# A decoder layer's output projection as seven products of halved matrices, with the summed and split weights made in the first SwiGLU's second phase

## The chip, the cores and the metric

The kernel runs on one core of one Trainium2 chip. The engines are TensorE (PE, matrix products), VectorE (DVE), ScalarE (ACT), GpSimd (POOL) and SyncE (SP, which here only issues transfers). The metric is the device time of one execution in microseconds. The kernel before takes 2163.99 us (median of 3 runs, 2163.88 to 2165.24).

## The reference, cut to what matters

```python
for l in range(DEPTH):                                  # DEPTH 1; x is 1 x 1024 x 1024, f32
    x = x + 0.5 * swiglu(rmsnorm(x, ffn1_norm[l]), ffn1_w_gu[l], ffn1_w_down[l])
    h = rmsnorm(x, mix_norm[l])
    z = h @ w_in[l]
    ...                                                 # y_a, y_b, y_c: three branches
    gates = jax.nn.sigmoid(z[..., COL_GATE:] + b_gate[l]).reshape(B, S, N_BRANCH, D_MODEL)
    merged = (gates[:, :, 0] * (y_a @ w_branch_a[l])
              + gates[:, :, 1] * (y_b @ w_branch_b[l])
              + gates[:, :, 2] * (y_c @ w_branch_c[l]))
    x = x + merged @ w_out[l]                           # the output projection, 1024 x 1024
    x = x + 0.5 * swiglu(rmsnorm(x, ffn2_norm[l]), ffn2_w_gu[l], ffn2_w_down[l])
```

## The kernel before

All activations are kept transposed: features on the 128 partitions, the 1024 tokens along the free dimension, in two halves of 512. A product of f32 matrices is three matmuls (`mm3`, L154): both operands are split into a rounded part (`whi`, a cast on ACT) and the rest (`wlo`, a subtraction on DVE), and the products hi by hi, hi by lo and lo by hi are summed in PSUM. `split` (L138) records such a cast and subtraction. A result of 128 x 512 fills one PSUM bank; there are four `bank` and four `one` (L127, taken by `single`).

The layer runs in stages: the first SwiGLU (`up` and `units`, then `down`), the gates' and latents' projections (`gates`), the three branches (`mixer`), the output projection (`project`), the second SwiGLU.

`down` (L2071) is the second phase of a SwiGLU. It computes a product of quartered matrices as seven loops (`loops`: b11, t3, t1, t2, b22, b21, t4), each of six steps `(n, s)`; five steps have two k tiles (24 matmuls of 512 columns) and one has one. Each step fetches the tiles of a later step (`fetch`: SP loads, `w_down` at L2109 and the other operand from `tdt` or `tdb` at L2111), splits the next step's operands (`prepare`, lines L139 and L142 in `split`), and runs what `acts` and `post` hang on it. `pre` and `post` carry the norm that follows and the start of the gates: `gates.first` (a load) and `gates.sums` (four additions on DVE). In this phase PE, SP, DVE and ACT run in the order of the code.

`mixer` (L1060) ends with sixteen products of the last branch, which fill `merged`, split into two parts as they come. `project` then makes sixteen outputs (2 halves x 8 blocks of 128 features), each a sum over 8 k tiles: 24 matmuls. For each it loads one 512 KB block of `w_out`, splits it, adds the bank to the residual (L1138) and feeds the norm: `norm.feed` squares on ACT and adds up on DVE (L1290). When half 0 is done, its norm is spread over the next outputs as `tasks`: `turned_sums` (four transposes on PE, L410, and a sum on DVE, L413), the steps of an inverse square root on DVE (L169 to L192, tiles `rms_v` and `rs_`), `norm_scale` (four transposes on PE, L425), and the product with the gains (L1327). Half 1's sums go by PE alone (L394). The order there is set by a scheduler for all engines.

## Time and profile before

| | |
|---|---|
| median of 3 runs | 2163.99 us (2163.88 to 2165.24) |
| profiled execution | 2163.42 us, span 2161.7 us |
| PE busy | 2152.9 us, 100% of the span |
| DVE, ACT, POOL busy | 1571.5, 911.7, 259.1 us |
| granted clock | 1.00 |
| data moved | 340.96 MB, 158 GB/s over the span |

Times in the trace are from the start of the span. The second phase of the first SwiGLU has its loop 2 from 499.5 us on and its loop 3 from 529.4. The last branch's sixteen products start at 1395.6, and the projection ends with the L425 transposes of half 1's norm at 1532.2. The page of the profile gives busy time, share and instructions for each engine, a map of 40 slices, the chain of work that ended last, and the costliest groups of instructions; a timeline row gives start, duration, engine, line, operation, output and inputs, and in square brackets the idle time before it and what ended it.

### The profile page before, as it was taken

The page shows a single profiled execution, that of the slowest core. Times are in us where ns is not written, and L with a number is a line of the kernel's source. Part 1 is how long each engine was busy: PE and PEld are TensorE (multiplying, and loading weights), DVE is VectorE, ACT ScalarE, POOL GpSimd, SP SyncE. Part 2 cuts the span into 40 slices and gives each one's busy share as a digit, 9 for nine tenths or more (in the row PEclk, how much of TensorE's full clock was granted, in tenths as well). Part 3 has the DMA queues.
Part 4 walks back from the last instruction along what each step waited for, and adds up shares of the span by engine and source line. Part 5 has one row for each costly group of instructions (what it writes and reads, how often), then busy time and mean ns, then how long its engine had stood idle before and what let it go on. Part 6 is the DMA issues. An engine that isn't in the chain of part 4 may idle for free.

```text
span 2161.7 us, 27485 instructions
## 1 busy us (share of the span) xinstructions
PE 2152.9 (100%) x10136; PEld 1798.9 (83%) x10136; DVE 1571.5 (73%) x2371; ACT 911.7 (42%) x1492; POOL 259.1 (12%) x268
## 2 busy tenths in 40 slices
PE   9999999999999999999999999999999999999999
PEld 6888888888887888888988899988888888888887
DVE  8966666679889657655886588876876666657884
ACT  6433333333455434443555378833433223224332
POOL 0011111100000000000123312240011212110000
PEclk9999999999999999999999999999999999999999
DMA  4264555385332444641687821192133332348543
GB/s 148 93 222 168 182 176 175 130 317 186 124 116 103 145 166 174 222 149 61 222 286 251 320 84 59 67 345 106 40 127 103 112 96 97 105 145 286 169 130 103
DMA packets 129975, 340.96 MB, mean 158 GB/s; under 512 B 15281, under 2 KB 23601, under 8 KB 129841
## 3 DMA queue, kind: packets, MB, share of 16 engines
q1 hardware_dynamic: 129696, 339.21, 45.5%
q8 instruction: 79, 1.29, 0.2%
q14 instruction: 56, 0.45, 0.1%
q10 hardware_dynamic: 144, 0.00, 0.0%
HBM read 229.33 MB, written 109.84 MB: 157 GB/s over the span
## 4 chain that ended last, share of the span: by engine, by line
PE 94%; DVE 4%; ACT 1%; issue 1%; DMA 0%; POOL 0%; ACTq 0%; POOLq 0%; DVEq 0%
PE one L158 15%; PE one L159 15%; PE one L160 15%; PE bank L158 13%; PE bank L159 13%; PE bank L160 13%; PE mm L158 2%; PE mm L159 2%; PE mm L160 2%; PE bank L1018 1%; PE bank L1033 1%; PE bank L1034 1%; PE bank L450 1%; DVE wlo L147 1%; PE bank L1950 1%; PE one L1950 1%
## 5 line engine op out<-in xcount | busy, mean ns | idle before, releaser
L146 ACT CAST whi<-x 128x1024 fp32r<-128x1024 f32 x202 | 192.2, 954 | 414.2 <-DVE x L1426 170.5
L147 DVE TENSOR_TENSOR wlo<-x,whi 128x1024 fp32r<-128x1024 f32 x202 | 241.3, 1196 | 59.2 <-ACT whi L146 19.4
L1454 DVE TENSOR_TENSOR t<-t,one 128x512 f32<-128x512 f32 x188 | 128.8, 685 | 192.3 <-PE one L160 192.2
L158 PE MATMUL bank<-h,whi 128*128 128x512 f32 x636 | 247.9, 390 | 0.0
L160 PE MATMUL bank<-h,wlo 128*128 128x512 f32 x636 | 247.5, 389 | 0.0
L159 PE MATMUL bank<-h,whi 128*128 128x512 f32 x636 | 247.5, 389 | 0.0
L158 PE MATMUL one<-h,whi 128*128 128x512 f32 x508 | 198.4, 391 | 0.0
L160 PE MATMUL one<-h,wlo 128*128 128x512 f32 x508 | 197.7, 389 | 0.0
L159 PE MATMUL one<-h,whi 128*128 128x512 f32 x508 | 197.7, 389 | 0.0
L158 PE MATMUL one<-w,whi 128*128 128x512 f32 x432 | 168.7, 390 | 0.1
L159 PE MATMUL one<-w,whi 128*128 128x512 f32 x432 | 168.1, 389 | 0.0
L160 PE MATMUL one<-w,wlo 128*128 128x512 f32 x432 | 168.1, 389 | 0.0
L142 DVE TENSOR_TENSOR wlo<-w,whi 128x1024 fp32r<-128x1024 f32 (+2 forms) x112 | 114.3, 1036 | 65.4 <-ACT whi L139 65.1
L139 ACT CAST whi<-w 128x1024 fp32r<-128x1024 f32 (+2 forms) x112 | 98.8, 902 | 148.5 <-PE one L159 63.9
L2050 POOL TENSOR_TENSOR raw<-raw 128x512 f32<-128x512 f32 x38 | 56.9, 1498 | 793.5 <-DVE raw L1891 685.0
L160 PEld LDWEIGHTS bank<-h,wlo 128*128 128x128 f32 x636 | 119.4, 188 | 25.0
L158 PEld LDWEIGHTS bank<-h,whi 128*128 128x128 f32 x636 | 119.4, 188 | 24.6
L159 PEld LDWEIGHTS bank<-h,whi 128*128 128x128 f32 x636 | 119.4, 188 | 24.4
L160 PE MATMUL bank<-whi,wlo 128*128 128x512 f32 x352 | 136.9, 389 | 0.0
L158 PE MATMUL bank<-whi 128*128 128x512 f32 x352 | 136.9, 389 | 0.0
L159 PE MATMUL bank<-wlo,whi 128*128 128x512 f32 x352 | 136.9, 389 | 0.0
L160 PEld LDWEIGHTS one<-h,wlo 128*128 128x128 f32 x508 | 95.3, 188 | 19.9
(406 smaller groups left out, 4902.7 us busy)
## 6 DMA issues: line engine op xcount, KB each, us to landing
x<-in_ffn_w_gu_dram SPq DMA_DIRECT2D x78, 512.0 KB, 5.1
w<-tdt SPq DMA_DIRECT2D x40, 512.0 KB, 4.6
gate<-raw SPq DMA_DIRECT2D x33, 512.0 KB, 3.0
tdb<-raw SPq DMA_DIRECT2D x64, 256.0 KB, 2.1
h<-in_ffn_w_down_dram SPq DMA_DIRECT2D x64, 256.0 KB, 6.0
w<-tdb SPq DMA_DIRECT2D x30, 512.0 KB, 4.5
tdt<-w SPq DMA_DIRECT2D x48, 256.0 KB, 2.3
x<-in_w_gate_dram SPq DMA_DIRECT2D x22, 512.0 KB, 7.0
```

What stands on the lines that cost most here:

```text
L139: i = self.nc.scalar.copy(hi, src)
L142: return (eng or self.nc.vector).tensor_tensor(lo, src, hi.bitcast(F32), op=ALU.subtract)
L146: self.nc.scalar.copy(hi, src)
L147: return lambda: self.nc.vector.tensor_tensor(lo, src, hi.bitcast(F32), op=ALU.subtract)
L158: i = mmul(out, s[0], m[0], start=first, stop=False, **kw)
L159: mmul(out, s[0], m[1], start=False, stop=False, **kw)
L160: self.last = mmul(out, s[1], m[0], start=False, stop=last, **kw)
L450: nc.tensor.transpose(b[:m, k * P:(k + 1) * P], s, self.ident)
L1018: nc.tensor.transpose(b[:, at:at + P], prs[t][:, kk * P:(kk + 1) * P], self.ident)
L1454: return self.nc.vector.tensor_tensor(out, x, y, op=ALU.add)
L1950: k.last = nc.tensor.matmul(b, w, norm.x(half, c), start=c == 0, stop=c == DT - 1)
L2050: sub = lambda d, x, y: (eng or nc.gpsimd).tensor_tensor(d, x, y, op=ALU.subtract)
```

## The change

Three things change. First, `merge` takes the place of `project`. It cuts `merged` (b11, b12, b21, b22) and `w_out` into quarters and makes seven products of four blocks with four k tiles each, 48 matmuls a product. Sums of quarters (t1 to t4) are made on DVE; product 1 (`p1`) is copied out of PSUM by ACT and added to the residual by POOL where it is needed; the others are added by DVE straight from PSUM (L1210), two of them after accumulating a second product in the same banks. PE's order in it is the code's; the other engines are ordered by the scheduler. The halves of the residual are stored and loaded the other way round.

Second, the seven weight matrices are made earlier. `out_jobs` makes fourteen jobs, two for each product. A job loads one quarter's half (512 KB), adds up to three further quarters with accumulating transfers issued by POOL, and four steps later splits the tile and stores both parts to `wo` in HBM. Job i starts at step 4 + i * 5 // 3 of the first SwiGLU's `down`, counted six to a loop. `merge` loads the parts back, 28 loads of 512 KB. Third, `gates.first(0)` and `gates.sums(0)` go from loop 1 to loop 5, and half 0's norm takes `one` banks for its transposes.

```diff
...
-        merged = [self.hrows() for _ in range(2)]
-        for _ in self.branch_pairs(
-                1, yb, mc, None, each, lambda d, f, x: self.split(*merged[f][d], x)):
-            pass
-        return merged
-
-    def project(self, merged, norm, sink):
-
...
+        return yb, mc
+    def out_jobs(self):
+        self.wo = self.dram.tile([7, 2, 2, P, D], F32, name="wo")
+        A11, A12, A22, A21 = range(4)
+        parts = ((A11,), (A11, A21, A22), (A21, A22), (A11, A21, A22, A12), (A11, A21), (A12,), (A22,))
+        def job(n, g):
+            x = self.raw()
+            src = self.a["w_out"][g]
+            self.nc.sync.dma_start(x, src[parts[n][0]])
+            for i in parts[n][1:]:
+                self.nc.gpsimd.dma_start(x, src[i], accum_op=ALU.add)
+            yield
+            hi = self.wide("whi")
+            lo = x.bitcast(F32R)
+            self.split(hi, lo, x)
+            for d, t in zip(self.wo[n, g], (hi, lo)):
+                self.nc.sync.dma_start(d, t.bitcast(F32))
+            yield
+        jobs = [job(n, g) for n in range(7) for g in range(2)]
+        when = {}
+        for i, j in enumerate(jobs):
+            q = 4 + i * 5 // 3
+            for at, k in ((q, 1), (q + 4, 0)):
+                at = when.setdefault((at // 6, at % 6), [])
+                at.insert(0 if k == 0 else len(at), lambda j=j: next(j))
+        return when
+    def merge(self, yb, mc, room, norm, load, sink):
+        nc, tt, h4 = self.nc, self.nc.vector.tensor_tensor, self.h4
+        names = ("b11", "b12", "b22", "b21")
+        raw = {n: [room() for _ in range(2)] for n in names}
+        w, op, x, banks = {}, {}, norm.x, {}
+        def put(name, p, src):
+            hi, lo = h4(F32R), h4(F32R)
+            op.setdefault(name, {})[p] = (hi, lo)
+            self.split(hi, lo, src)
+        def branch(name, k):
+            top, col = name[1] == "2", name[2] == "2"
+            dt, hf = 4 * top + k, int(col)
+            if dt not in w:
+                y = self.load(self.a["w_branch"][1, dt // 2])
+                w[dt], w[dt + 1] = y[:4], y[4:]
+            if k % 2 == 0:
+                branch.sig = self.x4()
+                for i in range(2):
+                    nc.sync.dma_start(branch.sig[:, i], self.sig[DT + dt + i][:, hf])
+            sig, m = branch.sig[:, k % 2], self.row()
+            nc.sync.dma_start(m, mc[dt][:, hf])
+            b = self.bank()
+            self.branch(b, w[dt], yb, hf)
+            tt(sig, sig, b, op=ALU.mult)
+            nc.gpsimd.tensor_tensor(raw[name][k // 2][:, k % 2], sig, m, op=ALU.add)
+        def weights(n):
+            out = []
+            for g in range(2):
+                ts = self.wide("whi"), self.wide("wlo")
+                for t, src in zip(ts, self.wo[n, g]):
+                    nc.sync.dma_start(t.bitcast(F32), src)
+                out += [tuple(t[:, u * 512:u * 512 + 512] for t in ts) for u in range(2)]
+            return out
+        def product(key, take, ws, name, first, last=True):
+            if first:
+                banks[key] = [None] * 4
+            for u in range(4):
+                if first:
+                    banks[key][u] = take()
+                for k in range(4):
+                    m = tuple(t[:, k % 2] for t in op[name][k // 2])
+                    s = tuple(t[:, k * P:(k + 1) * P] for t in ws[u])
+                    self.mm3(banks[key][u], s, m, first and k == 0, k == 3, skip_group_check=True)
+                yield u, banks[key][u]
+        def add(half, c, b, sign=ALU.add, parts=1):
+            y = x(half, c)
+            for n in self.parts(parts):
+                tt(y[:, n], y[:, n], b[:, n], op=sign)
+        for k in range(4):
+            branch("b11", k)
+            if k % 2:
+                put("b11", k // 2, raw["b11"][k // 2])
+        for k in range(4):
+            branch("b12", k)
+        ws = weights(0)
+        for k in range(4):
+            branch("b22", k)
+            if k % 2:
+                p = k // 2
+                b11, b12, b22 = (raw[n][p] for n in ("b11", "b12", "b22"))
+                tt(b12, b12, b22, op=ALU.subtract)
+                tt(b11, b12, b11, op=ALU.subtract)
+                put("t2", p, b11)
+        for k in range(4):
+            branch("b21", k)
+        load()
+        p1 = []
+        w2 = weights(1)
+        for u, b in product("a", self.single, ws, "b11", True):
+            p1.append(self.row())
+            nc.scalar.copy(p1[u], b)
+        for p in range(2):
+            b11, b22 = raw["b11"][p], raw["b22"][p]
+            put("b22", p, b22)
+            nc.vector.scalar_tensor_tensor(b22, in0=b22, scalar=-1.0, in1=b11, op0=ALU.mult, op1=ALU.subtract)
+        for p in range(2):
+            put("t1", p, raw["b22"][p])
+        ws = weights(2)
+        for u, b in product("x", self.bank, w2, "t2", True):
+            add(1, 2 * u + 1, b, ALU.subtract)
+        for u in range(4):
+            nc.gpsimd.tensor_tensor(x(0, 2 * u), x(0, 2 * u), p1[u], op=ALU.add)
+        for p in range(2):
+            put("t3", p, raw["b12"][p])
+        w2 = weights(3)
+        for u, b in product("x", None, ws, "t1", False):
+            add(0, 2 * u + 1, b, ALU.subtract)
+        for u in range(4):
+            nc.gpsimd.tensor_tensor(x(0, 2 * u + 1), x(0, 2 * u + 1), p1[u], op=ALU.subtract)
+        for p in range(2):
+            put("b21", p, raw["b21"][p])
+            tt(raw["b21"][p], raw["b21"][p], raw["b11"][p], op=ALU.add)
+        ws = weights(4)
+        for u, b in product("x", None, w2, "b22", False):
+            add(0, 2 * u, b)
+            norm.feed(0, 2 * u)
+        for u in range(4):
+            nc.gpsimd.tensor_tensor(x(1, 2 * u + 1), x(1, 2 * u + 1), p1[u], op=ALU.subtract)
+        for p in range(2):
+            put("t4", p, raw["b21"][p])
+        w2 = weights(5)
+        for u, b in product("y", self.bank, ws, "t3", True):
+            add(0, 2 * u + 1, b)
+            norm.feed(0, 2 * u + 1)
+            sink(0, 2 * u + 1)
+        ws = weights(6)
+        tasks, norm.take = [None, *norm.first()], self.single
+        for u, b in product("a", None, w2, "b21", False):
+            add(1, 2 * u, b)
+            norm.feed(1, 2 * u)
+            if u:
+                tasks[u]()
+        for u, b in product("y", None, ws, "t4", False):
+            parts = 2 if u == 3 else 1
+            if u == 0:
+                tasks[4]()
+                norm.take = None
+            add(1, 2 * u + 1, b, parts=parts)
+            norm.feed(1, 2 * u + 1, parts)
+            sink(1, 2 * u + 1)
...
-                    {(1, 0): [do(gates.first, 0)], (1, 4): [do(gates.sums, 0)],
+                    {(5, 0): [do(gates.first, 0)], (5, 2): [do(gates.sums, 0)],
                      (5, 3): [do(norm.high, 0), do(norm.low, 0)], (5, 4): [do(norm.apart, 0), do(gates.first, 1)],
...
-                    late)
+                    late, self.out_jobs())
...
-            merged = self.mixer(latents)
+            yb, mc = self.mixer(latents)
...
-            for half in range(2):
-                for p in range(DT // 2):
-                    nc.sync.dma_start(rows.take(half, p), x1d[half, p])
             norm = OpNorm(self, rows, lambda: self.g_ffn2)
             ffn = SwiGLU(self, a["ffn2_w_gu"], a["ffn2_w_down"], fp, norm, 2)
-            for f in range(2):
-                ffn.fetch(f, [ffn.w4] * 4)
-            self.project(merged, norm, lambda half, c: keep(x2d, norm.t, half, c))
+            def load():
+                for half, p in ((1, 0), (1, 1), (1, 2), (1, 3), (0, 0), (0, 1), (0, 2), (0, 3)):
+                    nc.sync.dma_start(rows.take(half, p), x1d[1 - half, p])
+            def sink(half, c):
+                if (half, c) == (0, 1):
+                    ffn.fetch(0, [ffn.w4] * 4)
+                elif (half, c) == (0, 3):
+                    ffn.fetch(1, [ffn.w4] * 4)
+                keep(x2d, norm.t, half, c)
+            with tc.manual_schedule(engines={mybir.EngineType.PE}):
+                self.merge(yb, mc, ffn.w4, norm, load, sink)
...
-            self.s[half] = k.turned_sums(self.acc.pop(half), late=True)
+            self.s[half] = k.turned_sums(self.acc.pop(half), late=True, bank=self.take)
...
-        self.s[half] = k.norm_scale(self.r[half], late=k.last is not None)
+        self.s[half] = k.norm_scale(self.r[half], late=k.last is not None, bank=self.take)
...
-                for act in [*acts[n, s], *post.get((n, s), ())]:
+                for act in [*acts[n, s], *post.get((n, s), ()), *jobs.get((n, s), ())]:
...
-    r["w_out"] = cols(i["w_out"].reshape(D, D), P)
+    w = i["w_out"].reshape(2, 4, P, 2, 2, 2, P).transpose(3, 5, 0, 2, 4, 1, 6)
+    w = np.stack([w[:, 0, 0], w[:, 0, 1], w[:, 1, 1], w[:, 1, 0]], 1)
+    r["w_out"] = c(w.reshape(2, 4, P, D))
```

What this does to the order of instructions, at the three places that matter. PE, at the end of the projection, between the transposes of half 0's squares and those of its scale. Before, the first and the last of the eight `mm3` of one output between them:

```order
L410 MATMUL bank<-ident,t 128x128 x4
L158 MATMUL bank<-h_12532,whi 128x512
L159 MATMUL bank<-h_12533,whi 128x512
L160 MATMUL bank<-h_12532,wlo 128x512
...
L158 MATMUL bank<-h_12538,whi 128x512
L159 MATMUL bank<-h_12539,whi 128x512
L160 MATMUL bank<-h_12538,wlo 128x512
L425 MATMUL bank<-ident,rs_y 128x128 x4
```

After, PE has the four `mm3` of the third block of the product with b21 there, into `one`:

```order
L410 MATMUL one<-ident,t 128x128 x4
L158 MATMUL one<-h_13259,whi 128x512
L159 MATMUL one<-h_13260,whi 128x512
L160 MATMUL one<-h_13259,wlo 128x512
...
L158 MATMUL one<-h_13264,whi 128x512
L159 MATMUL one<-h_13265,whi 128x512
L160 MATMUL one<-h_13264,wlo 128x512
L425 MATMUL one<-ident,rs_y 128x128 x4
L158 MATMUL one<-h_13259,whi 128x512
```

The transposes L410 and L425 have come from 24 matmuls to 12 apart. DVE at the same place; before, the sum of the squares, then the root with a split of weights ahead of it:

```order
L1138 TENSOR_TENSOR x_12915<-x_12915,bank 128x512
L413 TENSOR_REDUCE ts<-bank 128x4
L142 TENSOR_TENSOR wlo<-raw,whi 128x512 x2
L192 TENSOR_SCALAR rms_v<-ts 128x4
L169 TENSOR_SCALAR rs_y<-rms_v 128x4
L173 TENSOR_TENSOR rs_b<-rs_y 128x4
L175 SCALAR_TENSOR_TENSOR rs_w<-rs_b,rms_v 128x4
...
L185 SCALAR_TENSOR_TENSOR rs_y<-rs_w,rs_y 128x4
L1138 TENSOR_TENSOR x_12915<-x_12915,bank 128x512
L1327 SCALAR_TENSOR_TENSOR x_12911<-x_12911,c_ffn_norm,bank 128x512 x2
```

After, from the sum of the squares to the norm's product (L1436 is the old L1290, L1473 the old L1327); the add into `x_13021` reads the block that PE makes between L410 and L425:

```order
L413 TENSOR_REDUCE ts<-one 128x4
L147 TENSOR_TENSOR wlo<-w_13404,whi 128x1024
L192 TENSOR_SCALAR rms_v<-ts 128x4
L1436 TENSOR_TENSOR t<-t 128x512
L1210 TENSOR_TENSOR x_13021<-x_13021,one 128x512
L169 TENSOR_SCALAR rs_y<-rms_v 128x4
L173 TENSOR_TENSOR rs_b<-rs_y 128x4
...
L1436 TENSOR_TENSOR t<-t 128x512
L179 SCALAR_TENSOR_TENSOR rs_y<-rs_b,rs_y 128x4
...
L185 SCALAR_TENSOR_TENSOR rs_y<-rs_w,rs_y 128x4
L1473 SCALAR_TENSOR_TENSOR x_13029<-x_13029,c_ffn_norm,one 128x512 x2
```

Two adds of squares and one residual add now stand among the root's steps. DVE in `down`, loop 3's first step (`h` and `w` are the raw operands of the next steps, `raw` a weight quarter of `out_jobs`, `rope_q` a table for a later stage). Before:

```order
L142 TENSOR_TENSOR wlo<-w_4129,whi 128x1024
L2178 SCALAR_TENSOR_TENSOR x_3782<-bank,x_3782 128x512
L2178 SCALAR_TENSOR_TENSOR x_3870<-bank,x_3870 128x512
L354 TENSOR_TENSOR rope_q_3717<-t,rope_g_q 128x128
...
L2084 TENSOR_TENSOR h_3378<-h_3592,h_3378 128x512
L2084 TENSOR_TENSOR h_3380<-h_3594,h_3380 128x512
L142 TENSOR_TENSOR wlo<-h_3386,whi 128x512
L142 TENSOR_TENSOR wlo<-h_3388,whi 128x512
L142 TENSOR_TENSOR wlo<-w_4176,whi 128x1024
```

After, DVE at the same step, with the same neighbours:

```order
L142 TENSOR_TENSOR wlo<-w_4173,whi 128x1024
L2324 SCALAR_TENSOR_TENSOR x_3785<-bank,x_3785 128x512
L2324 SCALAR_TENSOR_TENSOR x_3887<-bank,x_3887 128x512
L142 TENSOR_TENSOR raw<-raw,whi 128x1024
L354 TENSOR_TENSOR rope_q_3716<-t,rope_g_q 128x128
...
L2230 TENSOR_TENSOR h_3379<-h_3593,h_3379 128x512
L2230 TENSOR_TENSOR h_3381<-h_3595,h_3381 128x512
L142 TENSOR_TENSOR wlo<-h_3387,whi 128x512
L142 TENSOR_TENSOR wlo<-h_3389,whi 128x512
L142 TENSOR_TENSOR wlo<-w_4225,whi 128x1024
```

One subtraction of 128 x 1024 has come in ahead of the rope table and of the next step's operands; it reads the seventh job's sum. SP in `down`, in loop 2, where before there are only operand loads:

```order
L2109 DMA w_3778<-in_ffn_w_down_dram 128x512
L2111 DMA w_4043<-tdt_1_99 128x512
L2111 DMA w_4086<-tdt_1_100 128x1024
L2111 DMA w_4129<-tdt_1_100 128x1024
L2111 DMA w_4176<-tdt_1_100 128x1024
```

After, stores of `wo` (which wait for a split) and loads of raw quarters stand between them:

```order
L2255 DMA w_3781<-in_ffn_w_down_dram 128x512
L2257 DMA w_4072<-tdt_1_99 128x512
L1141 DMA wo<-whi 128x1024
L1141 DMA wo<-raw 128x1024
L1133 DMA raw<-in_w_out_dram 128x1024
L2257 DMA w_4125<-tdt_1_100 128x1024
L1133 DMA raw<-in_w_out_dram 128x1024
L2257 DMA w_4173<-tdt_1_100 128x1024
L1141 DMA wo<-whi 128x1024
L1141 DMA wo<-raw 128x1024
L2257 DMA w_4225<-tdt_1_100 128x1024
```

Every operand load behind a store now waits for what that store waits for.

28 lines of the change are left out of this document (5 added, 23 removed).

## The prediction

> **What bounds the kernel now.** I read the page first: busy shares, then the slices.
>
> ```profile
> span 2161.7 us, 27485 instructions
> PE 2152.9 (100%) x10136; PEld 1798.9 (83%) x10136; DVE 1571.5 (73%) x2371; ACT 911.7 (42%) x1492; POOL 259.1 (12%) x268
> PE   9999999999999999999999999999999999999999
> DVE  8966666679889657655886588876876666657884
> ```
>
> TensorE (PE) has work in every slice, so the time is its work plus what it is made to wait. VectorE (DVE) stands at 8 and 9 tenths around slices 9 to 11, the first SwiGLU's second phase, where the change adds the weight work. So I took that stretch and the projection by windows (columns: length, then busy PE, PEld, DVE, ACT, POOL, clock, DMA share, GB/s).
>
> ```profile
> 490.00:520.00 30.00, 30.00 (x134) 24.86 (x133) 28.39 (x53) 10.59 (x15) 0.00 (x0) 1.00 0.64 224
> 520.00:550.00 30.00, 30.00 (x134) 24.86 (x133) 29.45 (x56) 12.96 (x21) 0.00 (x0) 1.00 0.37 103
> 550.00:580.00 30.00, 30.00 (x134) 24.82 (x134) 25.34 (x37) 13.17 (x20) 0.00 (x0) 1.00 0.40 127
> 1440.00:1500.00 60.00, 60.00 (x271) 49.66 (x270) 33.52 (x58) 19.37 (x35) 2.77 (x2) 1.00 0.52 194
> ```
>
> The granted clock is 1.00 throughout. In the projection (1440 to 1500) DVE is half idle; from 490 to 550 it has only 1.61 and 0.55 us to spare in 30. Last I took the timeline of PE (start, duration) for the price of a matmul and the end of the projection.
>
> ```profile
> 499.51 0.39 PE L158 MATMUL bank<-whi 128*128 128x512 f32 x1
> 529.43 0.39 PE L158 MATMUL one<-whi 128*128 128x512 f32 x1
> 1488.13 0.60 PE L410 MATMUL bank<-ident,t 128*128 128x128 f32 x4
> 1529.19 0.95 PE L394 MATMUL bank<-ones,t 128*128 128x1 f32 x8
> 1532.18 0.60 PE L425 MATMUL bank<-ident,rs_y 128*128 128x128 f32 x4
> ```
>
> **Matmuls saved.** The first two rows start loops 2 and 3 of the second phase: 29.92 us for 132 matmuls (11 k x 4 blocks x 3), 0.2267 us each. The projection has 16 x 8 x 3 = 384, the seven products 7 x 4 x 4 x 3 = 336: 48 fewer, **-10.9 us**, all on the path, since PE never idles there.
>
> **The end of the merge.** PE's order there is written out and does not bend. After the second block of the sixth product come the four L410 transposes of half 0's sum of squares, the third block (12 matmuls, 2.72 us), the four L425 transposes. Before, 24 matmuls (5.44 us) stood between. DVE's rows of before:
>
> ```profile
> 1488.33 0.69 DVE L1138 TENSOR_TENSOR x<-x,bank 128x512 f32<-128x512 f32 x1 [2.96 <-PE bank L160]
> 1488.94 0.68 DVE L413 TENSOR_REDUCE ts<-bank 128x4 f32<-128x512 f32 x1
> 1490.74 0.16 DVE L192 TENSOR_SCALAR rms_v<-ts 128x4 f32<-128x4 f32 x1
> 1492.32 0.16 DVE L185 SCALAR_TENSOR_TENSOR rs_y<-rs_w,rs_y 128x4 f32<-128x4 f32 x1
> 1527.35 0.75 DVE L1138 TENSOR_TENSOR x<-x,bank 128x256 f32<-128x256 f32 x2 [3.31 <-PE bank L160]
> 1528.31 0.76 DVE L1290 TENSOR_TENSOR t<-t 128x256 f32<-128x256 f32 x2 [0.21 <-ACT t L1285]
> 1531.83 1.22 DVE L147 TENSOR_TENSOR wlo<-w,whi 128x1024 fp32r<-128x1024 f32 x1
> 1532.96 2.71 DVE L1327 SCALAR_TENSOR_TENSOR x<-x,c_ffn_norm,bank 128x512 f32<-128x512 f32 x4
> 1535.60 2.48 DVE L147 TENSOR_TENSOR h<-x,h 128x1024 fp32r<-128x1024 f32 x2
> ```
>
> Start to start these give: a 512-wide operation 0.6 (1488.33 to 1488.94), a 1024-wide one 1.14 (1531.83 to 1532.96), a 512-wide of the norm 0.66 (2.64 for four), a step of the root 0.2 (1.58 for eight). In the changed order the residual add of that third block stands ahead of eight root steps, and a 512-wide add of squares among them. With L410's start as zero, PE ends the block at 0.44 + 2.72 = 3.2 and is at L425; DVE can only then start the add: 3.4 to 4.0, plus 8 x 0.2 + 0.6 = 2.2, so rs_y at 6.2 and L425 at 6.35. **First stall 3.2 us.**
>
> The L425 result reaches the norm 0.78 us later (1532.18 to 1532.96), at 7.1. From there DVE's order is unbroken work: 8 norm operations (5.3), 7 of 1024 (8.0), 6 of 512 (3.6), and the last block's add and squares (0.75 + 1.2 + 0.7, by the rows at 1527 and 1528), 19.5 us in all, to 26.6. PE has the fourth block, the four blocks of the seventh product and 9 matmuls of the next stage, 69 x 0.2267 + 0.44 = 16.1 after 6.35, so it stands at the L394 sums at 22.4, and these need the last square. **Second stall about 4.1 us**, of which some 1.3 comes already at an operand of those 9. From L394 on the order is the old one. The tail gives back 7.3. Its bounds: 3.2 if the norm's work were half covered, 9 if ACT's squares come late too.
>
> The rest of the merge I cost at nothing. The twelve adds on POOL have a like row in the page's costliest groups (busy, mean ns):
>
> ```profile
> L2050 POOL TENSOR_TENSOR raw<-raw 128x512 f32<-128x512 f32 x38 | 56.9, 1498 | 793.5 <-DVE raw L1891 685.0
> ```
>
> The cover is DVE's 26 us idle in the 60 of the window, and POOL's, which is busy for 2.77 there and gets 12 x 1.5 = 18. The 28 weight loads of 512 KB replace 16, four per product of 10.9 us, issued a product and a half ahead. If that cover went, a late load would hold the next product.
>
> **The weights in the second phase.** Fourteen splits: 1.05 on ACT (row below; ACT is busy 10.6 to 13.2 of 30, hidden) and 1.14 on DVE each. A step is 24 matmuls, 5.44 us; loop 3's steps 2 and 3 start at 540.31 and 545.75.
>
> ```profile
> 525.17 1.22 DVE L142 TENSOR_TENSOR wlo<-w,whi 128x1024 fp32r<-128x1024 f32 x1
> 530.47 1.23 DVE L142 TENSOR_TENSOR wlo<-w,whi 128x1024 fp32r<-128x1024 f32 x1
> 531.61 1.28 DVE L2178 SCALAR_TENSOR_TENSOR x<-bank,x 128x512 f32<-128x512 f32 x2
> 532.80 0.89 DVE L354 TENSOR_TENSOR rope_q<-t,rope_g_q 128x128 f32<-128x128 f32 x4
> 533.61 1.29 DVE L2084 TENSOR_TENSOR h<-h,h 128x512 f32<-128x512 f32 x2
> 534.82 1.28 DVE L142 TENSOR_TENSOR wlo<-h,whi 128x512 fp32r<-128x512 f32 x2
> 536.02 1.22 DVE L142 TENSOR_TENSOR wlo<-w,whi 128x1024 fp32r<-128x1024 f32 x1
> 541.57 1.21 DVE L142 TENSOR_TENSOR wlo<-w,whi 128x1024 fp32r<-128x1024 f32 x1
> 557.65 1.05 ACT L139 CAST whi<-w 128x1024 fp32r<-128x1024 f32 x1
> 607.82 1.29 DVE L142 TENSOR_TENSOR wlo<-w,whi 128x512 fp32r<-128x512 f32 x2 [2.22 <-ACT whi L139]
> ```
>
> The operands of steps 2 and 3 are ready at 537.24 and 542.78: slacks of 3.07 and 2.97. Per step DVE has 5.55 us of its own (530.47 to 536.02), so it never catches up. Five splits stand between loop 2's start and step 3's operands, 5.7 us, less the 1.61 idle of the first window: 4.1 against 2.97, a stall of **1.1** (0 if the sums taken out of loop 1 help, 2.7 if no idle is usable). The moved gate sums fall beside the 2.22 us gap before 607.82: nothing.
>
> **The accumulating transfers.** Fourteen DMAs on POOL's queue add quarters of the weight into a tile. Before has none, so their time t is open. The nearest rows by size (KB, us from issue to landing):
>
> ```profile
> raw<-in_w_out_dram SPq DMA_DIRECT2D x16, 512.0 KB, 4.9
> x2d<-x SPq DMA_DIRECT2D x8, 512.0 KB, 2.7
> w<-in_ffn_w_gu_dram SPq DMA_DIRECT2D x8, 512.0 KB, 9.9
> w<-tdt SPq DMA_DIRECT2D x40, 512.0 KB, 4.6
> ```
>
> Their bounds are 2.7 and 9.9; I take 4.9, the same matrix by the same kind of tile. It matters at the seventh job (product 4's first half), with three adds, each waiting for the one before. Its load stands in SP's queue behind the fifth job's stores, and these wait for its split, the last DVE work of loop 2's step 2: 499.51 + 2 x 5.44 + 5.55 + 1.14 = 517.1. The load lands 4.9 later at 522.0, and the sums are complete at 522.0 + 3t. Behind it, in ACT's and DVE's fixed order, stand the cast 1.05, the split 1.14, the rope 0.8 and the operands of step 2 (1.2 + 1.2 + 1.2): 6.6 us to be done by 540.31. That holds up to t = 3.9. At 4.9 step 2 is 3.0 late, and step 3, with 5.55 + 1.14 of DVE work against 5.44, another 1.25: **+4.3**, which contains the 1.1. At 2.7 it is +1.1; at 9.9 the first term is 18.0 and the whole +19.3. The tile for loop 3's own first step is queued in SP behind the same stores: 517.1 + 4.6 = 521.7, cast by 522.8, wanted at 525.17: in time by 2.4.
>
> The Trainium skill, page "DMA: Bandwidth & Descriptors", section "Anatomy of one DMA — SWDGE (gpsimd) path", gives for a DMA issued by GpSimd about 2.0 us plus the bytes at 436 GB/s; that makes an estimated 3.2 us here, by which the phase would cost +1.1 and the sum be -2.5. No row here shows such a transfer, and the loads of this size in the rows above are slower than that. By the page "SBUF — State Buffer", section "Who interferes with whom", such a transfer can also stand still while VectorE holds the port it shares with GpSimd, which would speak for a longer t in a stretch where VectorE is 95% busy.
>
> **Sum.** -10.9 + 7.3 + 4.3 = +0.7 on the profiled 2163.42 (span 2161.7 plus 1.7 around it): 2164.1. The median of the runs is 0.57 above that execution, so I say **2164.7**.
>
> **Rivals.** (A) As summed: 2161 to 2170. (B) *Slower*: the three chained adds hold ACT and DVE for long. Deciding point: +4.3 on the sum's other terms (-3.6) is +7.9 in the phase, t = 6.1; at 9.9 it is -3.6 + 19.3 = +16, 2180. For it: 512 KB loads in the DMA list take 4.9 to 9.9 when queues are full, and the window at 490 shows 224 GB/s. Against: 0.37 DMA share at 520. (C) *Faster*: the adds are quick and the second tail stall is mostly covered, because DVE's norm work starts before my 7.1 or runs into fewer waits: -10.9 + 3.2 + 1.1 = -6.6, 2157.4. For it: DVE half idle in the projection; against: the fixed order behind L425. (D) Merge loads come late: four loads at 9.9 in place of 4.9 lag a product by 5 us once or twice, +5 to +10, 2170 to 2175. For it: SP's queue also carries residual loads and stores; against: 0.52 DMA share.
>
> **Chances.** A 0.50, B 0.22, C 0.18, D 0.10. Faster or slower means by over 0.2%, 4.3 us, about what this measurement can tell. Faster: most of C and A's lower edge, 0.20; slower: B, D and A's upper edge, 0.31; within: 0.49. The range 2157 to 2176 leaves out the lower half of C and B beyond t = 9; A's own is 2161 to 2170.
>
> **What would show it.** Right: 0.2267 us per matmul in the merge; an L425 wait near 3 us on rs_y with the residual add ahead of it; an L394 wait near 3 to 4; waits of PE on wlo in loop 3 of the second phase, with the cast of the seventh job idle on a DMA. Wrong: no wait in loop 3 (t under 3.9), an L394 that starts at once, or waits inside the products on weight tiles. The forecast fails most likely through t.

## The result, and the profile after

The changed kernel takes 2198.43 us (median of 5 runs, 2198.05 to 2200.81) against 2164.10 before: a ratio of 1.016, 95% interval 1.0148 to 1.0171. That is 34.3 us slower, 22 us above the upper end of the forecast range. The side is that of rival B, the size is not.

The page of the changed kernel, the rows that answer to those of before, and with them the granted clock and the DMA share in 40 slices:

```profile
span 2196.7 us, 27531 instructions
PE 2155.5 (98%) x10088; PEld 1795.7 (82%) x10088; DVE 1591.2 (72%) x2367; ACT 915.6 (42%) x1476; POOL 293.8 (13%) x294
...
PE   9999999998799999999999999999999999999999
...
PEclk9999999999899999999999999999999999999999
DMA  4265554489962436553378650078033333338443
```

PE has 48 matmuls fewer, as counted, yet two slices are no longer full and one has a lower granted clock: slices 10 and 11, from 494 to 604 us. The windows there (columns as in the prediction):

```profile
490.00:520.00 30.00, 27.55 (x118) 21.53 (x116) 20.75 (x37) 10.12 (x15) 2.61 (x3) 1.00 1.04 334
520.00:550.00 30.00, 22.69 (x85) 17.02 (x85) 25.31 (x45) 11.84 (x18) 3.47 (x4) 0.89 1.01 337
550.00:580.00 30.00, 15.81 (x59) 12.29 (x60) 16.30 (x29) 9.21 (x12) 3.54 (x5) 0.77 1.00 280
```

PE runs 59 matmuls where 134 fit, and DVE, the engine that I had feared for, is idle half the time from 550 to 580. The DMA engines are full (1.00 to 1.04, against 0.37 to 0.64 before). What PE waits for (whole span; total, times, longest), and then what ACT and SP wait for between 470 and 660:

```profile
PE one L158 <- ACT whi L139: 11.9, 2, 11.3
PE bank L158 <- ACT whi L139: 4.7, 1, 4.7
PE one L159 <- DVE wlo L142: 4.3, 3, 2.8
PE bank L159 <- DVE wlo L142: 3.1, 4, 1.5
PE bank L410 <- DVE t L1436: 3.0, 1, 3.0
PE one L425 <- DVE rs_y L185: 3.0, 1, 3.0
PE bank L394 <- DVE t L1436: 2.4, 2, 2.3
```

```profile
ACT whi L139 <- DMA raw<-in_w_out_dram: 21.9, 2, 15.1
ACT whi L139 <- DMA wo<-whi: 21.5, 6, 4.9
```

```profile
SPq L1141 <- ACT whi L139: 32.8, 10, 12.1
SPq L1133 <- DMA wo<-raw: 32.7, 7, 8.9
```

The first five of PE's rows lie in the second phase and sum to 27.0 us. The phase loses 36.5 (below); the rest is matmuls that run slower behind the waits, at the granted clocks of 0.89 and 0.77 above.

The longest wait, 11.3 us, is at the place that the prediction named: the cast of the seventh job. Its transfers in POOL's timeline (L1135 are the accumulating ones; the seventh and eighth job with three each, taking turns, and in the last row the ninth job's), and the cast on ACT, with one of the fourth job ahead of it:

```profile
540.46 0.86 POOL L1135 DMA_DIRECT2D raw<-in_w_out_dram  x1 [13.87 <-DVE wlo L142]
543.08 0.88 POOL L1135 DMA_DIRECT2D raw<-in_w_out_dram  x1 [1.76 <-DMA raw<-in_w_out_dram]
547.20 0.87 POOL L1135 DMA_DIRECT2D raw<-in_w_out_dram  x1 [3.24 <-DMA raw<-in_w_out_dram]
552.22 0.86 POOL L1135 DMA_DIRECT2D raw<-in_w_out_dram  x1 [4.15 <-DMA raw<-in_w_out_dram]
556.38 0.86 POOL L1135 DMA_DIRECT2D raw<-in_w_out_dram  x1 [3.30 <-DMA raw<-in_w_out_dram]
561.22 1.78 POOL L1135 DMA_DIRECT2D raw<-in_w_out_dram  x2 [3.97 <-DMA raw<-in_w_out_dram]
```

```profile
518.90 1.04 ACT L139 CAST whi<-raw 128x1024 fp32r<-128x1024 f32 x1 [6.79 <-DMA raw<-in_w_out_dram]
563.79 1.04 ACT L139 CAST whi<-raw 128x1024 fp32r<-128x1024 f32 x1 [15.08 <-DMA raw<-in_w_out_dram]
```

The seventh job's chain began at 540.5, not at the 522.0 that I worked out, because the job's own load was issued by SP only at 532.9, behind stores and splits that were late already (its last 4.2 us of waiting were for the fourth job's store to free the tile):

```profile
532.92 0.33 SPq L1133 DMA_DIRECT2D raw<-in_w_out_dram  x1
```

The chain ended at 563.8. The first row of ACT is the same mechanism three jobs earlier: the fourth job's two additions held ACT until 518.9, DVE was busy for 0.02 of the 5 us from 515 to 520, and PE's wait of 4.7 us at 523.66 is behind that.

The places where time is gained and lost are fixed by three marks in PE's timeline: the first matmul of the last branch, half 1's sums L394 and its scale L425. The branch starts at 1432.75 in place of 1395.60: **+37.2 us**, 36.5 of them in the second phase, forecast +4.3. From there to L425 it is 134.6 us in place of 136.6: **-2.0**, forecast -3.6.

### The profile page after: what moved, and what is told of

Its sections match the earlier page's. It is cut to its first block, busy times and chain, and to the rows that moved or that the text cites. A ratio compares the mean times of both kernels' runs of the same rounds, so it can differ in the third digit from the quotient of the medians.

```text
span 2196.7 us, 27531 instructions
## 1 busy us (share of the span) xinstructions
PE 2155.5 (98%) x10088; PEld 1795.7 (82%) x10088; DVE 1591.2 (72%) x2367; ACT 915.6 (42%) x1476; POOL 293.8 (13%) x294
## 3 DMA queue, kind: packets, MB, share of 16 engines
q0 software_dynamic: 2016, 7.34, 1.8%
## 4 chain that ended last, share of the span: by engine, by line
PE 86%; DVE 7%; DMA 3%; ACT 1%; issue 1%; POOL 0%; SPq 0%; ACTq 0%; DVEq 0%; POOLq 0%
PE one L158 14%; PE one L159 14%; PE one L160 14%; PE bank L158 11%; PE bank L159 11%; PE bank L160 11%; DMA raw<-in_w_out_dram 2%; PE mm L158 2%; PE mm L159 2%; PE mm L160 2%; PE bank L1018 1%; DVE wlo L142 1%; PE bank L1033 1%; PE bank L1034 1%; PE bank L450 1%
## 5 line engine op out<-in xcount | busy, mean ns | idle before, releaser
L158 PE MATMUL bank<-h,whi 128*128 128x512 f32 x588 | 229.2, 390 | 0.0
L160 PE MATMUL bank<-h,wlo 128*128 128x512 f32 x588 | 228.8, 389 | 0.0
L159 PE MATMUL bank<-h,whi 128*128 128x512 f32 x588 | 228.8, 389 | 0.0
L158 PE MATMUL one<-h,whi 128*128 128x512 f32 x540 | 212.3, 393 | 0.0
L159 PE MATMUL one<-h,whi 128*128 128x512 f32 x540 | 211.4, 392 | 0.0
L160 PE MATMUL one<-h,wlo 128*128 128x512 f32 x540 | 211.4, 392 | 0.0
L158 PE MATMUL one<-w,whi 128*128 128x512 f32 x432 | 168.6, 390 | 0.4 <-DVE t L1600 0.4
L158 PE MATMUL bank<-whi 128*128 128x512 f32 x352 | 137.9, 392 | 4.7 <-ACT whi L139 4.7
L160 PEld LDWEIGHTS bank<-h,wlo 128*128 128x128 f32 x588 | 110.4, 188 | 23.1
L159 PEld LDWEIGHTS bank<-h,whi 128*128 128x128 f32 x588 | 110.4, 188 | 22.7
L158 PEld LDWEIGHTS bank<-h,whi 128*128 128x128 f32 x588 | 110.4, 188 | 22.6
L160 PEld LDWEIGHTS one<-h,wlo 128*128 128x128 f32 x540 | 102.1, 189 | 21.5
```

What stands on the lines that cost most here:

```text
L158: i = mmul(out, s[0], m[0], start=first, stop=False, **kw)
L159: mmul(out, s[0], m[1], start=False, stop=False, **kw)
L160: self.last = mmul(out, s[1], m[0], start=False, stop=last, **kw)
```

## The experiments

Each run is compared by its branch start (mostly the loss in the second phase) and by its time. Kernels whose second phase is the same gave branch starts that differ by up to 2.8 us (1396.5 to 1399.0 in the six with one job, 1396.1 to 1398.9 in the four with the phase of pool_late), so differences below that mean nothing.

Most of this spread arises far ahead of the phase: in seven of the traces (split_only, adds_plain and pool_late among them) matmuls near 41 us come every 0.43 us in place of 0.227, and these enter the phase 1.4 to 2.3 us late, the others 0.7 at most. Two marks in PE's timeline leave that out, the first L158 with `one<-x` behind 440 us and the L425 near the end of the phase. Before, they are

```profile
440.12 0.39 PE L158 MATMUL one<-x,whi 128*128 128x512 f32 x1
656.28 0.65 PE L425 MATMUL bank<-ident,rs_y 128*128 128x128 f32 x4 [0.66 <-DVE rs_y L185]
```

216.2 us apart, and after the change 252.7 (440.80 to 693.49): 36.5 us more. I call this the loss inside the phase. The six kernels with one job agree in it to 0.1 us (all 0.8), the four with the phase of pool_late to 1.0 (0.2 to 1.2).

**The merge alone, the additions, the stores.** Four edits; the first three are

```diff
-        jobs = [job(n, g) for n in range(7) for g in range(2)]     # m_only
+        jobs = [job(0, 0)]
-                for t, src in zip(ts, self.wo[n, g]):              # m_only, no_store
+                for t, src in zip(ts, self.wo[0, 0]):
-            for i in parts[n][1:]:                                 # no_adds
-                self.nc.gpsimd.dma_start(x, src[i], accum_op=ALU.add)
-            for d, t in zip(self.wo[n, g], (hi, lo)):              # no_store
+            for d, t in zip(self.wo[n, g], (hi, lo)) if n + g == 0 else ():
```

and the fourth, pool_jobs, makes the sums alone in the second phase, with loads, accumulating transfers and stores all in POOL's queue (one chain for products 3, 2 and 4, one for product 5, for each half), and loads and splits fourteen unsplit weights in the merge.

> Only one of the fourteen weight jobs is left (at loop 4, without additions), and the merge reads that one weight for every product, so the output is not the reference's; the merge's instructions and loads are as in the change. Measured for the change: the second phase of the first SwiGLU lost 37.2 us (first matmul of the last branch at 1432.8 in place of 1395.6) and the merge gained 2.0 (134.6 us against 136.6). Every theory of the loss in that phase says that it goes with the jobs: the branch starts within 2 us of 1395.6, and the time is 2162, between 2160 and 2164. If the merge alone were slower than the old projection, it would be over 2166.

Measured: 2163.96 (ratio 0.9998, 0.9988 to 1.0007), branch start 1396.97 (+1.4, inside the phase 0.8), merge 135.7 us. The loss of the second phase does go with the jobs. The merge by itself brings no measurable change.

> The fourteen accumulating transfers are left out (the weight sums are then single quarters, so the output is not the reference's); loads, splits and stores stay. Theory C (the chains of accumulating transfers hold the cast and all behind it on ACT and DVE): 25 or more of the 37 us go, the time is at most 2172. Theory R (the stores to HBM hold the five whi buffers, the three raw buffers and SP's queue): the loss stays over 20 us, time 2183 or more. Both together: about 2176.

Measured: 2173.66, branch start 1406.88 (+11.3, inside the phase 11.2). Theory C, though the time is 1.7 over the bound that I had set: 25.9 of the 37.2 us (inside the phase 25.3 of 36.5) go with the fourteen accumulating transfers.

> All stores of the weight parts but the first job's two are left out, and the merge reads that one for every product (output not the reference's); loads, accumulating transfers and splits stay. Theory C: the chains still hold ACT, loss over 20 us, time 2183 or more. Theory R: at most 2172, and ACT no longer waits for a store to release whi. Both together: about 2176.

Measured: 2194.72, branch start 1427.63 (+32.0, inside the phase 31.5). Theory R falls as the main cause; the waits on `wo<-whi` and `wo<-raw` above are real, but without the stores 5.0 us go.

> The sums alone are made in the second phase, by loads, accumulating transfers and stores that all stand in POOL's queue (20 transfers of 512 KB, nothing on SP, ACT or DVE); the merge loads fourteen unsplit weights and splits them itself. Theories C and R agree that transfers which hold no engine and no buffer of the phase cost nothing: branch start within 2 us of 1395.6. The merge then has 14 x 1.14 = 16 us more of DVE work and half the weight traffic; with DVE idle for 14 us of 60 in it: time 2161 to 2166. If the added bytes alone slow the phase's own loads, over 2170.

Measured: 2188.77 (ratio 1.0112, 1.0097 to 1.0127), branch start 1416.47 (+20.9, inside the phase 19.4). Both theories had said that transfers which hold no engine and no buffer cost nothing; they cost about 19 us. The transfers began at 452 us, where the phase's own loads are densest, and the wait shifted to these (between 450 and 520 the phase's 512 KB loads `w<-tdt` took a median of 16.0 us to land, 6.4 before): ACT between 450 and 680, then the window.

```profile
ACT whi L139 <- DMA w<-tdt: 35.2, 7, 9.2
```

```profile
480.00:510.00 30.00, 23.19 (x83) 17.30 (x82) 13.48 (x23) 8.38 (x13) 6.53 (x10) 0.83 1.05 338
```

Two new theories came from this: that the bytes as such fill the DMA engines, and that an accumulating transfer takes them for longer than a plain one.

**Bytes, waits, accumulation.** The edits, each on the changed kernel:

```diff
-                self.nc.gpsimd.dma_start(x, src[i], accum_op=ALU.add)
+                self.nc.gpsimd.dma_start(x, src[i])                        # adds_plain
+                self.nc.gpsimd.dma_start(self.aside[n, g, i][:, :64], x[:, :64])   # adds_aside, both lines
+                self.nc.gpsimd.dma_start(self.aside[n, g, i], src[i])
```

`aside` is an unused place in HBM. split_only is no_adds with the stores left out as in no_store.

> The fourteen accumulating transfers become plain loads of the same bytes from the same queue with the same waits (each overwrites the tile, so the output is not the reference's). Losses so far, by the first matmul of the last branch against 1395.6: the change +37.2, without stores +32.0, without the accumulating transfers +11.3, without jobs +1.4. Theory D (an accumulating transfer takes the DMA engines about twice as long per byte, in a stretch where they are already full): the loss falls to 25 or less, time 2184 or less. Theory L (what counts is that each link of a chain waits for the one before to land, whatever it does): the loss stays at 33 or more, time 2192 or more.

Measured: 2190.24, branch start 1424.54 (+28.9, inside the phase 26.7), between the two. The queues between 430 and 640 (packets, MB, time as a share of 16 engines; q0 holds POOL's transfers), first of the changed kernel, then of this one:

```profile
q1 hardware_dynamic: 20847, 58.64, 75.0%
q0 software_dynamic: 2016, 7.34, 18.5%
```

```profile
q1 hardware_dynamic: 21386, 60.22, 77.8%
q0 software_dynamic: 2016, 7.34, 9.5%
```

The same 2016 packets and 7.34 MB take the engines 18.5% of this stretch when they accumulate and 9.5% when they do not (from 460 to 580 the DMA share is 0.96 to 1.04 in the change and 0.88 to 1.02 here). Their time from issue to landing:

```profile
raw<-in_w_out_dram POOLq DMA_DIRECT2D x14, 512.0 KB, 8.5
```

```profile
raw<-in_w_out_dram POOLq DMA_DIRECT2D x14, 512.0 KB, 4.9
```

> The fourteen accumulating transfers become copies of the same 512 KB from the weight to an unused place in HBM, from the same queue, each started once its job's tile has landed (by a small store of 64 columns); no cast or split waits for them, and the weights are single quarters, so the output is not the reference's. Branch start so far, against 1395.6: splits alone +12.0, all but the additions +11.3, additions as plain loads into the tile +28.9, the change +37.2. Theory W (the wait for a chain of landings holds ACT and DVE): the loss stays at 11 to 15, time 2174 to 2178. Theory B (the bytes fill the DMA engines, and the phase's own loads come late): 22 or more, time 2184 or more.

Measured: 2184.23, branch start 1418.56 (+23.0, inside the phase 22.3). Theory B, at its lower edge: no engine but POOL waits for these copies, and they still cost 11.7 us over no_adds (inside the phase 11.1). (They write to HBM where the others write to the tile, and are issued in larger groups, so this is the price of about these bytes, not of exactly these.)

> No accumulating transfers and no stores but the first job's two; the merge reads that one weight throughout (output not the reference's). Fourteen loads and fourteen splits stay. If DVE's backlog from the splits were the cause of what is left without the additions (+11.3), the loss stays at 8 or more, time 2171 or more. By the forecast's own term for the backlog (1.1, and about 2 at the moved sums) it is 1 to 5, time 2164 to 2168, and the rest of the 11.3 is the stores'.

Measured: 2173.63, branch start 1407.61 (+12.0). The phase itself lost 9.5, since this execution entered it 2.3 late. By that, the stores without the additions cost 1.8 (no_adds 11.2), and thirteen more jobs of one load and one split cost 8.7 more than the one of m_only. The moved sums are in both. PE's waits:

```profile
PE bank L410 <- DVE t L1434: 2.7, 1, 2.7
...
PE one L159 <- DVE wlo L142: 1.4, 2, 1.0
PE bank L159 <- DVE wlo L142: 1.2, 2, 0.9
```

Every one of them ends on DVE. They are spread from 525 us to 610, and matmuls behind a wait can be slower, of which below: the wait of L410 and the slow matmuls behind it make up 4.7 of the 9.5.

> As the kernel with loads and splits alone (branch start +12.0, 2173.6), with the fourteen low parts subtracted by POOL in place of DVE; POOL is idle there. If DVE's backlog made the loss: the branch starts at +1 to +5, time 2164 to 2168. If it was ACT's casts or the loads: it stays at +10 or more. POOL's own subtraction of two SBUF tiles may slow DVE's by its port: between the two.

The edit to split_only is `self.split(hi, lo, x, self.nc.gpsimd)`. Measured: 2181.58, branch start 1414.75 (+19.2, inside the phase 18.5): worse. POOL's subtractions (first row) take twice DVE's, and DVE's own grow: an operation that meets one (second row; the same takes 0.22 us in split_only), and the groups of 512-wide low parts between 480 and 640, here and then in split_only.

```profile
483.12 2.43 POOL L142 TENSOR_TENSOR raw<-raw,whi 128x1024 fp32r<-128x1024 f32 x1 [31.74 <-ACT whi L139]
483.20 2.42 DVE L301 TENSOR_SCALAR t<-t 128x128 f32<-128x128 f32 x1
```

```profile
L142 DVE TENSOR_TENSOR wlo<-h,whi 128x512 fp32r<-128x512 f32 x45 | 38.4, 888 | 4.7 <-ACT whi L139 4.7
```

```profile
L142 DVE TENSOR_TENSOR wlo<-h,whi 128x512 fp32r<-128x512 f32 x48 | 31.1, 684 | 2.1 <-ACT whi L139 2.1
```

The mean goes from 684 to 888 ns, but not evenly: five of the 45 take 1.58 to 2.88 us, the others stay near 684 ns. The five are among the operations that start while POOL subtracts and end only with it. ACT also waits 15.6 us for POOL to release `whi`, where in split_only it waits 3.3 for DVE. So this does not answer whether a free DVE would have removed the 8.7; that PE waits for DVE's low parts is seen, the rest is argued.

> As the kernel with all transfers in POOL's queue (2188.8; branch start +20.9, merge 141.1 us in place of 135.7), with the first transfer held back until loop 3 of the second phase, where before the DMA engines were 0.35 to 0.48 busy (in place of 0.87). Theory D: the loss in the phase goes, branch start within 2.5 us of 1395.6, time 2167 to 2170. If transfers of this queue cost the phase something wherever they stand: over 2176.

pool_late holds the chains of pool_jobs back, each by a one-column addition on POOL that reads an operand of a step, from the last of loop 2 to step 4 of loop 3. Measured: 2171.34 (ratio 1.0030, 1.0019 to 1.0041), 1.3 over what I had written, branch start 1398.89 (+3.3). Inside the phase it lost 1.2, where pool_jobs lost 19.4. The windows:

```profile
520.00:550.00 30.00, 30.00 (x134) 24.84 (x133) 28.13 (x52) 13.03 (x21) 8.46 (x12) 1.00 0.77 213
550.00:580.00 30.00, 29.65 (x130) 23.99 (x129) 21.86 (x33) 11.68 (x18) 7.38 (x12) 1.00 1.02 300
```

The same twenty transfers that cost 19 us from 452 on cost next to nothing 70 us later. They fill the DMA engines here too (1.02), but the phase needs little of them, and no engine but POOL waits for the chains. The rest of the time is the merge: 142.7 us in place of 135.7. DVE now also splits the weights there, and PE waits for its residual adds and root (1.2 at L410 and 4.2 at L425, in place of 0 and 3.0).

**Where the merge's 10.9 us go.** In m_only the ideal is 136.6 - 10.9 = 125.7 us; it takes 135.7. The first stall and the end in PE's timeline:

```profile
1506.72 0.65 PE L425 MATMUL one<-ident,rs_y 128*128 128x128 f32 x4 [3.00 <-DVE rs_y L185]
...
1523.77 0.50 PE L159 MATMUL one<-h,whi 128*128 128x512 f32 x1 [1.16 <-DVE h L147]
...
1526.96 1.87 PE L394 MATMUL bank<-ones,t 128*128 128x1 f32 x8 [2.46 <-DVE t L1436]
...
1529.26 0.63 PE L159 MATMUL one<-h,whi 128*128 128x512 f32 x1
1529.69 0.63 PE L160 MATMUL one<-h,wlo 128*128 128x512 f32 x1
...
1532.67 0.60 PE L425 MATMUL bank<-ident,rs_y 128*128 128x128 f32 x4
```

Besides the waits (3.0 at the first L425, 1.2, 2.5), the rows behind the last one tell of a cost that I had not reckoned: matmuls of 0.63 in place of 0.39 us, one every 0.43 in place of 0.227, and the eight small L394 in 1.87 in place of 0.95. The granted clock there is 0.79:

```profile
1520.00:1530.00 10.00, 6.38 (x25) 4.97 (x24) 8.00 (x18) 2.06 (x5) 0.00 (x0) 0.79 0.47 186
```

From L394 to the last L425 it is 5.71 us in place of 2.99 before (1529.19 to 1532.18), 2.7 more; with the waits, 9.3 of the 10.0.

Three other orders of the end were tried on m_only, two of them also on pool_late. In all three DVE runs in the order of the code there. m_tail puts the tasks (root and scale) ahead of the add; the others are, cut to what matters,

```diff
         for u, b in product("a", None, w2, "b21", False):             # m_tail3, m_tail4
+            if u == 2:
+                tasks[2]()
+                tasks[3]()
             add(1, 2 * u, b)
+            if u == 1:
+                tasks[1]()
             norm.feed(1, 2 * u)
-            if u:
-                tasks[u]()
+            if u == 3:
+                tasks[4]()
...
-            norm.feed(1, 2 * u + 1, parts)
+            (norm.square(1, 2 * u + 1).keep if u > 1 else ...)()      # m_tail, m_tail3
-                    turn=5, third=..., count=2)
+                    turn=8, third=..., count=5)                       # m_tail; 7 and 4 in m_tail3, m_tail4
```

> As the kernel with one job (2163.96), with another order at the end of the merge: half 0's root comes ahead of the residual adds on DVE, DVE's order is the code's there, the last two squares of half 1 go to PE's sums without additions on DVE, and these sums stand 6 units of 3 matmuls further down, their scale 3 units. The merge lost 10.0 us of its 10.9 there: 135.7 us from the branch's start to the end, against 136.6 - 10.9 = 125.7. If it is the order, 5 to 9 of them come back, time 2155 to 2159. If DVE simply has too much work there, the wait moves on to the operands of half 1 and less than 3 come back, over 2161.

Measured: 2168.16 (ratio 1.0017, 1.0007 to 1.0026). The L425 wait falls to 0.9 and L394's to 0.4, and PE then waits 3.3 for a cast of half 0.

> As the kernel with one job, with the end of the merge in a third order: the residual add of the block before L410 ahead of the root, half 0's first norm part right behind L425, its second after the last block of that product, the last two squares of half 1 summed by PE, and these sums after 5 units in place of 3. The first try (2168.2) took the L425 wait from 3.0 to 0.9 and the L394 wait from 2.7 to 0.4, but PE waited 3.3 for a cast of half 0's part, whose norm stood behind two more adds. If order decides: no wait over 1.5 before L394, merge from 135.7 to 129 to 132 us, time 2158 to 2162. If DVE's work is too much in any order: 2163 or more.

Measured: 2168.89 (1.0017, 1.0008 to 1.0026). One more order, the same time.

> As the kernel with one job, with nothing changed but the last three squares of half 1, which go to PE's sums (twelve more small matmuls of one column) in place of three additions on DVE: 1.9 us off the end of DVE's unbroken work. By the forecast's reading of the second stall the L394 wait falls from 2.7 to about 1: 1 to 3 us faster, 2161 to 2163. If other work takes its place at once: no change.

Measured: 2167.31 (1.0010, 1.0001 to 1.0020). The L394 wait does fall, to 0.5, and L394 itself grows:

```profile
1525.22 5.71 PE L394 MATMUL bank<-ones,t 128*128 128x1 f32 x26 [0.49 <-ACT t L1431]
...
1531.36 0.63 PE L159 MATMUL one<-h,whi 128*128 128x512 f32 x1
```

There are 32 small matmuls in place of 8, where I had expected twelve more. Twenty-six of them take 5.71 us, and the nine matmuls behind them are at half rate, though those ahead were at the full one (0.40 us at 1523.64): small matmuls did not keep the rate. More was lost than 1.9 us of DVE work.

> As the kernel with one job, in the third order of the merge's end, but with half 1's squares all added on DVE as before (8 small L394 matmuls; the squares left to PE made 24 more of about 0.22 us each, at half rate, and kept the matmuls behind them at half rate too). The sums stand after 5 units in place of 3. If the squares on PE were what the other orders lost by: 2157 to 2162, with the L425 wait near 1.3 and an L394 wait under 1.5. If DVE's work is too much in any order: the L394 wait grows to 3 or more, 2163 or more.

Measured: 2168.16 (1.0018, 1.0008 to 1.0027). Without the kept squares the L394 wait grows to 3.9. The orders move one wait between three places; the squares on PE were not what they lost by.

> As the kernel with one job (2163.96), without six of the eight residual adds of the merge's last two products (the output is not the reference's): 6 x 0.6 = 3.6 us less DVE work, and the add that waits for the block between L410 and L425 is gone. PE, its order and the loads are the same. If DVE's work in this stretch is what the merge loses its gain to, the L425 wait of 3.0 goes to under 1 and the L394 wait of 2.7 to under 1, with the half-rate matmuls behind them: 5 to 9 us faster than the kernel with one job, 2155 to 2159. If the loss sits elsewhere: less than 3 us.

Measured: 2159.25 (0.9977, 0.9967 to 0.9986), merge 130.2 us. With 3.6 us less DVE work, the L425 wait is 1.3 and L394's 1.8, and 4.7 us come back in the time, 5.5 in the merge. So the adds at the end, their work on DVE and the wait of one of them for PE's block, account for about half of the 10.0; where the other half would go is not shown. The L394 wait was to go under 1 and did not, and the time just misses the 2155 to 2159 that I had written.

> The complete computation: sums by POOL's queue from loop 3 on (2171.3, branch start +3.3, merge 142.7 us with its fourteen splits), with the end of the merge in the third order. If the order brings what it brings in the kernel with one job: 2165 to 2168. If the splits in the merge leave DVE no room, little is gained: over 2169.

Measured: 2177.01 (1.0052, 1.0037 to 1.0067): over 2169, and a loss where I had written little gain.

> As the one before, with six sums of quarters of the branches (128 x 1024) on POOL in place of DVE: 6 x 1.14 = 7 us less DVE work in the merge, about 6 x 3 us more on POOL, which is 19 of 30 us busy there. If DVE is what the merge waits for: 2 to 5 us faster than the one before. If POOL is late for t2 or takes DVE's time by its port: no gain or a loss.

Measured: 2179.87 (1.0064, 1.0047 to 1.0081), a loss: POOL with 7 us of DVE's additions is no relief.

> The complete computation: sums by POOL's queue from loop 3 on and splits in the merge (2171.3), with the end of the merge as in the run beside it. It should gain on 2171.3 what that run gains on 2164.0, less what the splits take from DVE at the same place: 2165 to 2170. Over 2171 if the order brings nothing with the splits there.

Measured: 2176.98 (1.0059, 1.0044 to 1.0074), a loss as well. No complete version beat the kernel before; the best of them is pool_late at 2171.34.

## Why the prediction was wrong, step by step

I forecast no measurable change, and it became 34 us slower. Two terms failed: the accumulating transfers, and the splits. Each row below is a kernel against the next simpler one:

| us | branch start | inside the phase |
|---|---|---|
| one job and the moved sums (m_only) | 1.4 | 0.8 |
| thirteen more loads and splits (split_only over m_only) | 10.6 | 8.7 |
| stores (no_adds over split_only) | -0.7 | 1.8 |
| bytes of fourteen more transfers (adds_aside over no_adds) | 11.7 | 11.1 |
| waiting for their chains (adds_plain over adds_aside) | 6.0 | 4.4 |
| that they accumulate (the change over adds_plain) | 8.2 | 9.8 |
| sum (of the unrounded) | 37.2 | 36.5 |

Every row rests on one trace of each kernel, and the parts are not independent: inside the phase the additions cost 22.0 without the stores and 25.3 with them. By the branch starts the first row and the stores lie within the spread; inside the phase the stores' 1.8 is barely above it.

- **Matmuls saved**, -10.9: right in count and pitch. Of it the merge kept 2.0 in the change and 0.9 in m_only.
- **The end of the merge**, +7.3: the mechanism was right, each at its place. The first stall was 3.0 (forecast 3.2), the second 2.3 at L394 (forecast 4.1 together with an operand). Mis-sized by the half-rate matmuls behind the stalls: in the change they add 1.6 behind the first, and from L394 to L425 it is 4.65 us in place of 2.99. The whole end gave back 8.9 there, in m_only 10.0.
- **The splits**, +1.1: the term was mis-sized eightfold (8.7 with their loads; PE's waits there all end on DVE, but how much is the loads' is not shown). I took two deadlines, loop 3's steps 2 and 3, and stopped. split_only shows the first wait in loop 2 already (0.9 us at 524.9), and six more splits behind my two steps, each on a DVE that had 24 to 29 us of 30 in use, ending with a 2.7 us wait of L410 for the squares of half 0's norm. The sums that were moved to loop 5, which I costed at nothing, stand there too; alone they cost 0.8 at most (m_only).
- **The accumulating transfers**, t = 4.9: this was the step that failed. A plain transfer in that place does take 4.9; an accumulating one took 8.5, below my upper bound of 9.9. But I counted them as a delay in one chain and not as load on the DMA engines: against the +4.3, which held the splits' 1.1 too, they cost 25.3, and 11.1 of that comes from the bytes alone with no engine of the phase waiting for them. The window at 490 with a DMA share of 0.64 was in front of me, and I read 0.37 at 520 as an argument against rival B. I also let the chain matter at the seventh job only, with the fifth job's split done at 517.1; the fourth job's additions held it up already, and the fifth's split came at 527.0. The jobs add loads, additions and stores of 512 KB from 457 us on, ahead of that. I did not open these windows of before:

```profile
430.00:460.00 30.00, 30.00 (x134) 24.85 (x133) 23.96 (x30) 11.54 (x17) 5.13 (x3) 1.00 0.88 322
460.00:490.00 30.00, 30.00 (x135) 24.82 (x134) 21.43 (x37) 13.43 (x21) 0.00 (x0) 1.00 0.87 313
```

With a DMA share of 0.87 there, everything behind them in SP's queue comes late; the seventh job's load was issued at 532.9, where I had 517.1.
- **The Trainium skill**, page "DMA: Bandwidth & Descriptors", section "Anatomy of one DMA — SWDGE (gpsimd) path", gives a fit from which I estimated 3.2 us for t. The trace differs: 4.9 for plain and 8.5 for accumulating ones in this full stretch. By the Trainium skill, page "SBUF — State Buffer", section "Who interferes with whom", two-input work on VectorE contends with GpSimd's reads. Nothing here shows that this port held the transfers: POOL's own rows for them above are 0.9 us each, and between them POOL mostly waits for a landing. split_pool agrees with the contention, with 888 ns for 684.
- **Rival B** had the right side and, with t = 8.5, would have come to about +11 in place of +34: the same missing load. That the side was B's is in part luck, since the load and the splits brought most of it. **Rival D** (late loads) I had placed in the merge only; the late loads were in the second phase.

## What to carry to other kernels

Work that is put "beside" other work needs a free engine, a free queue and free DMA engines in that very stretch: add the bytes of a moved step to the DMA share of its window before reading its latency from a row. A chain of accumulating transfers was dear where the phase's own loads kept the DMA engines 0.87 busy (19.4 us), and nearly free some 70 us later where they were 0.37 to 0.48 busy (1.2 us), with a queue for itself in both. And where PE is saved time by handing sums to DVE, find the stretch in which DVE has no gap, since saved matmuls come back as waits there.

## What was not expected of the hardware

- An accumulating transfer took the DMA engines twice as long per byte as a plain one of the same packets: 18.5% against 9.5% of the same 210 us for 7.34 MB, in a stretch where the DMA share was 0.88 to 1.04.
- In split_pool, DVE operations on SBUF that started while POOL subtracted ended only with the subtraction, one of them after 2.42 us in place of 0.22; this is seen at thirteen of POOL's fourteen subtractions, and at the other POOL itself took 5.06 us in place of some 2.4. Adds on DVE that read a bank of PSUM (`x<-bank,x`) ran at their 0.68 us meanwhile. A mean of 888 ns hides this.
- Behind a wait, PE's matmuls could come every 0.43 us in place of 0.227, some 8 of them: in the change behind the waits of 2.96 us (L425) and 2.28 us (L394). It did not happen each time. The twelve matmuls behind the first of these take, with L425, 4.84 us in the change and 3.26 in m_only, whose wait of 3.00 us is as long; so the same stall cost about 4.5 us in one and 3.0 in the other. Small matmuls of one column did not keep the rate up: in m_keep no wait near them was over 1.2 us, 26 of them took 5.71 us, and the nine matmuls behind were slow. In the change, behind the first 5 us wait of the second phase, the granted clock was 0.55:

```profile
525.00:530.00 5.00, 4.02 (x10) 3.19 (x11) 4.93 (x9) 0.59 (x2) 0.86 (x1) 0.55 1.03 379
```

The Trainium skill, page "TensorE: Matmul & The Clock Gate", section "Part 1: The HAM clock gate (the "warmup" mystery)", tells of such a gate, with half the clock after an idle window of about 3.4 us and the full one again after as long a busy stretch. The trace agrees on the half rate; a wait of 2.28 us was enough to bring it on in the change, and one of 3.00 us in m_only was not. My sum had no term for it, and a stall in it can need one.
